# The low part of each weight block by a negating copy and an accumulating transfer, in a one-core diffusion step

## The chip, the cores and the metric

The kernel runs on one core of one Trainium2 chip. The metric is the device time in microseconds. Three runs of the kernel before took 1739.32, 1740.16 and 1740.61 us, so its time is the median, 1740.16 us.

## The reference

The reference is one inference step of a hybrid backbone with two layers (model width 1024, 512 latent and 128 context tokens, all in float32). Only its large products matter here; the mixers between the two projections (a gated delta rule in chunks, a spatial gating, a pooling) are left out.

```python
h = rmsnorm(x, norm1_g) * (1 + sc1) + sh1
cols = h @ w_in                      # 1024 x 2832, three groups of heads behind it
x = x + g1 * (concat(ya, yb, yc) @ w_out)      # 1024 x 1024
h = rmsnorm(x, norm2_g) * (1 + sc2) + sh2
gate, up = split(h @ w_gu)           # 1024 x 5632
x = x + g2 * ((silu(gate) * up) @ w_down)      # 2816 x 1024
```

The modulation (sh, sc, g) is a product of SiLU of a condition vector with w_mod (1024 x 6144 in each layer), once for the context and once for the latent tokens.

## The kernel before

All 640 tokens are kept transposed: features on the 128 partitions, tokens along the row. A product runs on 128 output features at a time. Its weight block is 1024 x 128 (768 x 128 in the last third of w_down), brought to one tile of 128 partitions with 8 (or 6) blocks side by side. The tokens go through in two halves of 320 columns.

TensorE multiplies float32 in a reduced form (float32r), so each operand is kept as two parts, hi and lo, whose sum is the value. A product is three passes: hi by hi, hi of the weights by lo of the tokens, lo of the weights by hi of the tokens (`mm3`, line 335). The lo part of a weight block, `wl`, is thus first needed by the third pass of the first block.

`wblock` (line 329) brings a block in and splits it. `wload` (line 297) issues the load of the raw weights into `w32` (called w in the profile) on SP's queue, all weight loads in the order of the program. `wsplit_` (line 311) then makes the parts: ScalarE casts the raw tile into `wh` (line 322); VectorE subtracts wh from the raw weights for the first 5 blocks (or 3), GpSimd for the last 3 (`GW`), into `wl` (lines 324 to 326; VectorE's operations all show as line 122). There are two buffers each of w32, wh and wl (`W32`, `WHL`). A buffer of wh or wl is written again when TensorE has done the last product that reads it, one of w32 when the subtractions have read it.

The modulation is worked off in small steps between the products (`pump_`, line 257): a load of 128 x 512 weights on SP's queue (line 268), a multiply-add on VectorE, a scaling on ScalarE in place, an addition on GpSimd (line 282) that also frees the buffer. There are three such buffers (`WM`). In the trace the additions all lie before 810 us, in the first layer.

The order on each engine's queue comes from the order of the program, moved by offsets (`at`, `PRI`; "split" is 70 earlier). Every engine takes its queue in order, and an instruction that waits holds up those behind it. The layers come one after the other: input projection with the mixers, output projection, feed-forward with 44 gate and up pairs in three pieces, each followed by its part of w_down.

Of the kernel before, what the change touches and what calls it, by code (L numbers as in the profile page):

```python
# [10 lines left out]
F32R = mybir.dt.float32r  # L11
# [6 lines left out]
P = 128  # L18
# [14 lines left out]
# steps of the modulation after each half of a product, by branch  # L33
PUMPS = {'log0': (0, 0), 'k00': (0, 0), 'q00': (1, 2), 'sgu0': (1, 1), 'z0': (0, 1), 'v10': (1, 1), 'q10': (0, 0), 'v00': (1, 0), 'k10': (0, 1), 'pool0': (1, 0)}
# engines of single steps: a ScalarE, v VectorE, p GpSimdE
ENG = {"gul11": "a", "kd10": "a", "conv_k01": "a", "conv_v10": "v", "gul00": "v", "mtc10": "v", "pumpmix0": "a", "kd11": "v", "gul01": "v", "mtc01": "a", "conv_q00": "v", "conv_v00": "v", "kd00": "a", "conv_q10": "a", "conv_k00": "v", "conv_q11": "a", "conv_v01": "a", "conv_v11": "a", "gul10": "a", "kn11": "a", "kn01": "a", "msb": "v", "pumpout0": "a", "dec01": "a", "conv_k11": "a", "dec00": "s", "pumpffn0": "a", "mtc11": "v", "mtc00": "a", "kd01": "a"}
GW, NB = 3, 2
# offsets in the order of issue: > 0 earlier
PRI = {"first": 1000, "rst": 80, "inverse10": 2000, "queries11": -230, "po": 240, "opost00": 180, "chain00": -220, "keys00": 530, "values00": -420, "br0": 200, "prep01": -170, "split": 70, "opost10": -30, "prep10": 430, "values11": 220, "chain11": 1000, "chain10": 10, "inverse01": 420, "keys10": 200, "evac": -10, "opost11": 50, "chain01": -300, "keys11": -100, "queries10": 130, "kept": -1000, "conv": -70, "br1": 10, "add": -100, "opost01": 100, "prep00": 50, "inverse11": -10, "values10": -30}
W32, WM, WHL = 2, 3, 2  # L40
# [5 lines left out]
def host_constants():  # L46
    f = np.float32
    p = np.arange(P)
    cols = {}
    cols["ones"] = np.ones((P, P), f)  # L50
    cols["U0"] = (p[:, None] <= p[None, :]).astype(f)
    cols["U1"] = (p[:, None] >= p[None, :]).astype(f)
    r, q = p[:, None] % 32, np.arange(32)[None, :]
    cols["MK"] = ((r >= 16) != (q >= 16)).astype(f)
    cols["I16"] = (p[:, None] % 16 == np.arange(16)[None, :]).astype(f)
    cols["m16"] = np.stack([p % 32 < 16, p % 32 >= 16], 1).astype(f)
    # from here on: not kept on chip as they are
    cols["ident"] = np.eye(P, dtype=f)
    cols["NID"] = np.eye(P, dtype=f) * f(NEG)
    cols["V0"] = (p[:, None] > p[None, :]).astype(f)  # L60
    cols["V1"] = (p[:, None] < p[None, :]).astype(f)
    quarter = D // 4
    omega = (f(1.0) / (f(10000.0) ** (np.arange(quarter, dtype=f) / f(quarter)))).astype(f)
    rr = np.arange(NL // GRID_W, dtype=f)[:, None] * omega
    cl = np.arange(GRID_W, dtype=f)[:, None] * omega
    row = np.concatenate([np.sin(rr), np.cos(rr)], -1).astype(f)
    col = np.concatenate([np.sin(cl), np.cos(cl)], -1).astype(f)
    for k in range(4):
        cols[f"row{k}"] = np.ascontiguousarray(row[:, k * P:(k + 1) * P].T)
        cols[f"col{k}"] = np.ascontiguousarray(col[:, k * P:(k + 1) * P].T)  # L70
    for nm, seg in (("l", GRID_W), ("c", P)):
        for g, win in enumerate(POOL_WINDOWS):
            b = np.zeros((P, P), f)
            for t in range(P):
                s0, pos = t // seg * seg, t % seg
                lo = min(max(pos - win // 2, 0), seg)
                hi = min(max(pos + win - win // 2, 0), seg)
                b[t, s0 + lo:s0 + hi] = f(1) / f(hi - lo)
                b[t, t] -= f(1)
            cols[f"B{nm}{g}"] = np.ascontiguousarray(b.T)  # L80
    off, o = {}, 0
    for k, v in cols.items():
        off[k] = (o, v.shape[1])
        o += v.shape[1]
    return np.ascontiguousarray(np.concatenate(list(cols.values()), axis=1)), off
# [6 lines left out]
def tile_hybrid_step(ctx: ExitStack, tc: tile.TileContext,  # L92
# [40 lines left out]
    def times(key, o, i, c, default):  # L133
        """o = i * c, c one number per row"""
        e = ENG.get(key, default)
        if e == "a":
            act(o, i, AF.Copy, scale=c)
        elif e == "v":
            ts(o, i, c, None, MUL)
        else:  # L140
            nc.gpsimd.tensor_scalar(o, i, c, None, op0=MUL)
# [10 lines left out]
    class at:  # L152
        """the instructions inside come that much earlier in the order of issue"""
# [11 lines left out]
    def behind(ins, prev):  # L165
        """queues one instruction of an engine behind another"""
        if prev is not None:
            tc.add_manual_dep(ins, prev.name, mybir.DependencyInfo(mybir.DependencyClass.NoSync,
                                                                   mybir.DependencyReason.DATA), reason="queue order")
# [7 lines left out]
    def in_turn(key, ins):  # L177
        """instructions of one kind in the order of the program"""
        behind(ins, recent.get(key))
        recent[key] = ins  # L180
# [38 lines left out]
    # steps: 512 columns x 128 rows of w_mod; a step's load is issued some steps ahead of its arithmetic  # L219
# [4 lines left out]
    def mod_sums(l, c0, ma):  # L224
# [11 lines left out]
        # sums over the 32 rows of each quarter, then over the quarters  # L236
# [50 lines left out]
    def pump_to(l, w):  # L287
        """until that sixth of the modulation is there"""
        n = 2 * KT * (SIXTHS.index((l, w)) + 1)
        while ps_["i"] < n:  # L290
            pump()
        if ps_["i"] == n and ps_["due"] is not None:
            mod_sums(*ps_["due"])
            ps_["due"] = None

# [1 line left out]
    def wload(parts, kn, n):  # L297
        """parts: [(dram [rows, n], k0, kn)] -> [P, kn, n]"""
# [7 lines left out]
    def wsplit(v):  # L306
        """hi, lo as blocks [P, n]"""
        with at("split"):
            return wsplit_(v)

    def wsplit_(v):
        kn, n = v.shape[1:]
        wh = wp.tile([P, 1024], F32R, tag="wH", name="wh", bufs=WHL)
        wl = wp.tile([P, 1024], F32R, tag="wL", name="wl", bufs=WHL)
# [8 lines left out]
        c = kn - GW  # L323
        tt(wl[:, 0:c], v[:, 0:c], wh[:, 0:c], SUB)
        if GW:
            nc.gpsimd.tensor_tensor(wl[:, c:], v[:, c:], wh[:, c:], op=SUB)  # L326
# [13 lines left out]
    def mmk(o, wb, k, xk, sl):  # L340
        """one k block of the products with the scaled residual; 16 columns: hi and lo in one operand"""
# [6 lines left out]
    def gemm_xs(wb, xs, evac, pumps=(1, 1), done=None):  # L348
        """products with the scaled residual; the first half carries two shift columns in front.
        done: the second half's, where it came first."""  # L350
# [28 lines left out]
    def rsqrt(y, a, t):  # L379
        """y = 1 / sqrt(a) for small tiles: bit shift, then three Newton steps; t: scratch like y."""  # L380
# [8 lines left out]
    class Norm:  # L389
        """scaled residual split in two, and the row statistics of the plain one."""  # L390
# [33 lines left out]
        def rstd(self, after=None):  # L424
            """per row: [row in chunk, chunk]"""
# [30 lines left out]
    wsp = tc.alloc_tile_pool(name="wsh", bufs=1, side="right")  # L456
    with tc.tile_pool(name="xin", bufs=1) as xp:
# [27 lines left out]
        def first_w(pool, j, c0, kp=KT):  # L485
            """512 columns of w_mod; the row blocks from kp on in the tiles of the later steps"""
# [7 lines left out]
        def first_mod(ws, c0, pool=None):  # L494
            """four row blocks side by side"""
            with at("first"):
                first_mod_(ws, c0, pool)
# [38 lines left out]
        # feature rows, positions added  # L536
# [35 lines left out]
        for k in range(KT):  # L572
# [5 lines left out]
            # sums of squares in two strands  # L578
# [18 lines left out]
    # ================= layers =================  # L597
    for l in range(DEPTH):
        xs = nrm.xs
        with ExitStack() as es:  # L600
            pa_, pb_ = (es.enter_context(tc.tile_pool(name=f"{t}{l}", bufs=1, reuse_waits="tile")) for t in ("ma", "mb"))
            # what the scans leave first lies where the residual comes back to
# [3 lines left out]
            if l == 0:  # L606
                # until the shift is there: halves of the first products that don't carry it
# [5 lines left out]
                def kept(w, t, c0):  # L613
                    """split into the tiles t, from column c0 of the first (hi) and the third (lo) on"""
# [79 lines left out]
            # beta = 1 / (1 + exp(-x)), kept negated  # L694
# [5 lines left out]
            # g = -exp(a_log) * softplus(alpha + dt_bias)  # L700
# [53 lines left out]
            def row_sums(b, so, i, t, dst=None):  # L754
                """sums of squares over each row of t; its natural layout in dst"""
# [10 lines left out]
            def keys(b):  # L766
# [6 lines left out]
                # kst: norm of k, its inverse square, and what the q norm leaves in the eps of the output norm  # L773
# [39 lines left out]
            # unit u = d * 10 + chunk * 2 + head  # L813
# [48 lines left out]
            def inverse(b):  # L862
                """MT holds -M^T (M strictly lower / upper); becomes (I + M)^-T in place."""
# [23 lines left out]
                for j in range(15):  # L887
# [7 lines left out]
                    else:  # L895
                        # few columns: float32 itself
# [4 lines left out]
                # forward units: Z = Y blocks; backward units: Z = X blocks  # L901
# [10 lines left out]
                # 16 -> 32: a forward and a backward unit share a tile, on different halves of its rows  # L912
# [27 lines left out]
                # diagonal 32-blocks of the result  # L940
# [5 lines left out]
                # 32 -> 64: forward and backward units share columns, on different partitions  # L946
# [32 lines left out]
                # 64 -> 128  # L979
# [21 lines left out]
            def chain(b):  # L1001
# [5 lines left out]
                for s in range(NCH):  # L1007
# [11 lines left out]
                    # scaled k, natural layout  # L1019
# [18 lines left out]
                    # (context units: vw = -v_new)  # L1038
# [73 lines left out]
            def to_nat(src, dst):  # L1112
                """two transposed tiles [128 ch, tokens] -> natural [128 tok, (chunk, 256)] in dst (two tiles of 3, 2 chunks)."""
# [9 lines left out]
            def mixt():  # L1123
                """tiles for the operands of the output projection, in place of what the scans have left."""
# [156 lines left out]
        mark(f"out{l}")  # L1281
        with tc.tile_pool(name=f"fx{l}", bufs=1, reuse_waits="tile") as xpool, tc.tile_pool(name=f"ft{l}", bufs=1, reuse_waits="tile") as ftp, tc.tile_pool(name=f"ff{l}", bufs=1, reuse_waits="tile") as fp:
# [25 lines left out]
            for pi_, fn in enumerate(pieces):  # L1308
# [23 lines left out]
                elif last:  # L1332
                    # back to natural layout, the final norm's statistics on the way
# [5 lines left out]
                    # both parts of the tokens use the same weights; they stay in tiles that the gate left  # L1339
# [97 lines left out]
```

## Time and profile before

| | before |
|---|---|
| median of the runs | 1740.16 us |
| profiled execution, first to last instruction (span) | 1737.7 us |
| TensorE busy | 1666.4 us (96%) |
| VectorE busy | 1155.2 us (66%) |
| ScalarE busy | 761.1 us (44%) |
| GpSimd busy | 585.3 us (34%) |
| mean granted TensorE clock | 0.987 |
| transfers of GpSimd's queue | 1152 packets, 2.51 MB |

The profile is of one execution. The runs were timed without it; the span lies 2.5 us under their median. PE is TensorE's matrix products, PEld its weight loads, DVE VectorE, ACT ScalarE, POOL GpSimd, SP the engine that only issues transfers; a q behind an engine means its queue. Products follow each other every 0.15 us while each is shown with some 0.31 us, since they overlap. An arrow in brackets names what ended an engine's idle time.

### The profile page before, as it was taken

How to read it: one execution, taken by the hardware profiler on the slowest of the kernel's cores; microseconds unless marked ns; L12 is line 12 of the kernel's file. 1: busy time of each engine (PE TensorE's matmuls, PEld its weight loads, DVE VectorE, ACT ScalarE, POOL GpSimd, SP SyncE). 2: the span in 40 equal slices, each digit the busy share in tenths (PEclk: the TensorE clock that was granted, in tenths of full speed). 3: DMA queues.
4: the chain of work that ended last, by engine and by line, in shares of the span. 5: the costliest groups of instructions: out<-in, count | busy, mean ns of one | idle time of the engine just before them, and what ended most of it. 6: DMA issues, size and time to landing. Idle time of an engine off the chain costs nothing.

```text
span 1737.7 us, 33153 instructions
## 1 busy us (share of the span) xinstructions
PE 1666.4 (96%) x12952; PEld 1603.2 (92%) x12952; DVE 1155.2 (66%) x2462; ACT 761.1 (44%) x1564; POOL 585.3 (34%) x578
## 2 busy tenths in 40 slices
PE   6999999998899999999999999999999999999997
PEld 4788989988899999999998899999999999999997
DVE  6698688799888688877467777675544434433454
ACT  4557765554444344434246656543322212321232
POOL 3342330367645454554164112013411221222110
PEclk8999999999999999999999999999999999999999
DMA  9431231444444544453241211113222222222221
GB/s 316 143 98 57 68 99 29 150 127 139 145 141 141 154 137 143 143 158 103 62 144 52 62 38 50 37 51 126 83 73 74 79 79 74 74 73 73 74 85 61
DMA packets 243379, 174.34 MB, mean 100 GB/s; under 512 B 10006, under 2 KB 212376, under 8 KB 243224
## 3 DMA queue, kind: packets, MB, share of 16 engines
q1 hardware_dynamic: 231888, 157.44, 29.8%
q10 hardware_dynamic: 10184, 12.29, 2.2%
q0 software_dynamic: 1152, 2.51, 0.4%
q8 instruction: 102, 1.67, 0.4%
q14 instruction: 53, 0.43, 0.1%
HBM read 163.29 MB, written 8.91 MB: 99 GB/s over the span
## 4 chain that ended last, share of the span: by engine, by line
PE 53%; DVE 3%; ACT 1%; issue 1%; POOL 0%; DMA 0%; DVEq 0%; POOLq 0%; ACTq 0%
PE acc L117 47%; PE dl L117 5%; DVE wl L122 0%; PE md L117 0%; DMA w<-in_w_down_dram 0%; PE dl L1379 0%; DVE cv L125 0%; POOL guh L830 0%; PE md L760 0%; DVE yt L125 0%; DVE st L125 0%; DVE Z L122 0%; ACT wh L322 0%; ACT MT L945 0%; DVE SI L122 0%
## 5 line engine op out<-in xcount | busy, mean ns | idle before, releaser
L117 PE MATMUL acc<-xhi,wh 128*128 128x322 f32 (+2 forms) x2112 | 667.4, 316 | 5.4 <-DVE ga L122 4.6
L117 PE MATMUL acc<-xlo,wh 128*128 128x322 f32 (+2 forms) x2112 | 666.0, 316 | 1.4 <-DVE xlo L125 1.2
L117 PE MATMUL acc<-xhi,wl 128*128 128x320 f32 (+1 forms) x2080 | 655.0, 315 | 5.1 <-DVE wl L122 5.1
L326 POOL TENSOR_TENSOR wl<-w,wh 128x384 fp32r<-128x384 f32 x188 | 258.7, 1376 | 792.5 <-ACT wh L322 777.9
L117 PEld LDWEIGHTS acc<-xhi,wh 128*128 128x128 f32 (+1 forms) x2112 | 399.4, 189 | 10.7 <-PE acc L117 7.2
L117 PEld LDWEIGHTS acc<-xlo,wh 128*128 128x128 f32 (+1 forms) x2112 | 400.2, 189 | 4.1 <-POOL spp L1148 1.5
L117 PEld LDWEIGHTS acc<-xhi,wl 128*128 128x128 f32 x2080 | 396.4, 191 | 6.6 <-DVE wl L122 5.9
L322 ACT CAST wh<-w 128x1024 fp32r<-128x1024 f32 (+1 forms) x188 | 194.5, 1035 | 343.4 <-PE acc L117 282.6
L282 POOL TENSOR_TENSOR ma<-ma,wm 128x512 f32<-128x512 f32 x140 | 207.2, 1480 | 133.5 <-ACT wm L150 113.8
L122 DVE TENSOR_TENSOR wl<-w,wh 128x640 fp32r<-128x640 f32 (+1 forms) x188 | 213.3, 1134 | 50.5 <-ACT wh L322 23.9
L117 PE MATMUL acc<-ah,wh 128*128 128x320 f32 (+2 forms) x632 | 195.6, 309 | 0.7 <-ACT ah L1322 0.7
L117 PE MATMUL acc<-al,wh 128*128 128x320 f32 (+2 forms) x632 | 195.1, 309 | 0.1
L117 PE MATMUL acc<-ah,wl 128*128 128x320 f32 (+2 forms) x632 | 195.1, 309 | 0.0
L150 ACT ACTIVATE wm<-wm,sc 128x512 f32<-128x512 f32 x140 | 101.1, 723 | 135.0 <-DVE ma L125 117.8
L125 DVE SCALAR_TENSOR_TENSOR x<-acc,mod,x 128x128 f32<-128x128 f32 (+3 forms) x192 | 77.9, 434 | 119.8 <-PE acc L117 119.5
L125 DVE SCALAR_TENSOR_TENSOR ma<-wm,sc,ma 128x512 f32<-128x512 f32 x140 | 134.9, 964 | 25.6 <-DMA wm<-in_w_mod_dram 24.7
L117 PEld LDWEIGHTS acc<-ah,wh 128*128 128x128 f32 x632 | 118.7, 188 | 1.2 <-ACT ah L1322 1.1
L117 PEld LDWEIGHTS acc<-al,wh 128*128 128x128 f32 x632 | 118.7, 188 | 0.3 <-DVE al L122 0.3
L117 PEld LDWEIGHTS acc<-ah,wl 128*128 128x128 f32 x632 | 118.7, 188 | 0.0
L1322 ACT CAST ah<-ga 128x320 fp32r<-128x320 f32 x88 | 40.5, 460 | 155.9 <-DVE ga L125 155.9
L150 ACT ACTIVATE ga<-ga,bt 128x320 f32<-128x320 f32 x132 | 57.4, 468 | 89.9 <-DVE ga L122 89.9
L122 DVE TENSOR_TENSOR ga<-acc,rst 128x320 f32<-128x320 f32 x88 | 42.4, 483 | 73.9 <-PE acc L117 73.4
(369 smaller groups left out, 2481.7 us busy)
## 6 DMA issues: line engine op xcount, KB each, us to landing
w<-in_w_gu_dram SPq DMA_DIRECT2D x88, 512.0 KB, 3.7
wm<-in_w_mod_dram SPq DMA_DIRECT2D x162, 256.0 KB, 2.9
w<-in_w_in_dram SPq DMA_DIRECT2D x44, 512.0 KB, 3.6
w<-in_w_down_dram SPq DMA_DIRECT2D x32, 512.0 KB, 4.2
w<-in_w_out_dram SPq DMA_DIRECT2D x32, 256.0 KB, 3.0
wf<-in_w_mod_dram SPq DMA_DIRECT2D x30, 256.0 KB, 6.5
w<-in_w_down_dram SPq DMA_DIRECT2D x16, 384.0 KB, 3.4
x<-xd ACTq DMA_DIRECT2D x16, 320.0 KB, 4.7
```

Of the source, the lines that this page charges most:

```text
L117: return nc.tensor.matmul(o, lhsT=l, rhs=r, start=st, stop=sp, **kw).ins
L122: recent["v"] = nc.vector.tensor_tensor(o, a, b, op=op).ins
L125: recent["v"] = nc.vector.scalar_tensor_tensor(o, a, s, b, op0=op0, op1=op1).ins
L150: recent["a"] = nc.scalar.activation(o, i, f, **kw).ins
L282: nc.gpsimd.tensor_tensor(ma[:, 1], ma[:, 1], wm, op=ADD)
L322: nc.scalar.copy(wh, v)
L326: nc.gpsimd.tensor_tensor(wl[:, c:], v[:, c:], wh[:, c:], op=SUB)
L1322: nc.scalar.copy(hi[:, sl], ga[:, sl])
```

## The change

In `wsplit_` the two subtractions go. ScalarE, behind the cast, copies the raw weights a second time with a scale of -1 into wl, which is float32r like wh and so holds minus hi. Then a transfer issued by GpSimd adds the raw tile to wl, from SBUF to SBUF. The number of buffers of wl has a name of its own (`WL`) and stays two. The other lines of the diff drop comments.

```diff
-GW, NB = 3, 2
+NB = 2
...
-W32, WM, WHL = 2, 3, 2
+W32, WM, WHL, WL = 2, 3, 2, 2
...
-        wl = wp.tile([P, 1024], F32R, tag="wL", name="wl", bufs=WHL)
+        wl = wp.tile([P, 1024], F32R, tag="wL", name="wl", bufs=WL)
...
         nc.scalar.copy(wh, v)
-        c = kn - GW
-        tt(wl[:, 0:c], v[:, 0:c], wh[:, 0:c], SUB)
-        if GW:
-            nc.gpsimd.tensor_tensor(wl[:, c:], v[:, c:], wh[:, c:], op=SUB)
+        act(wl, v, AF.Copy, scale=-1.0)
+        nc.gpsimd.dma_start(wl, v, accum_op=ADD)
         return tuple([t[:, k, :] for k in range(kn)] for t in (wh, wl))
```

## Rows read from the trace of the kernel before

**Rows 1.** The page, part 1: busy us, share of the span, instructions.

```profile
PE 1666.4 (96%) x12952; PEld 1603.2 (92%) x12952; DVE 1155.2 (66%) x2462; ACT 761.1 (44%) x1564; POOL 585.3 (34%) x578
```

**Rows 2.** The page, part 4: the chain that ended last, share by engine.

```profile
PE 53%; DVE 3%; ACT 1%; issue 1%; POOL 0%; DMA 0%; DVEq 0%; POOLq 0%; ACTq 0%
```

**Rows 3.** Windows: length, busy of PE, PEld, DVE, ACT, POOL (count), clock, DMA share, GB/s.

```profile
390.00:520.00 130.00, 117.98 (x774) 113.84 (x773) 115.38 (x175) 58.38 (x94) 79.42 (x61) 0.97 0.46 142
...
1210.00:1670.00 460.00, 459.26 (x3102) 458.02 (x3101) 199.32 (x392) 123.52 (x192) 106.61 (x81) 1.00 0.25 75
450.00:470.00 20.00, 16.50 (x107) 16.21 (x104) 18.84 (x27) 8.74 (x14) 11.92 (x9) 0.91 0.49 156
```

**Rows 4.** Windows of line 322 (the cast) alone: length, ACT busy (count), clock, DMA.

```profile
1210.00:1670.00 460.00, 68.06 (x65) 1.00 0.25 75
```

**Rows 5.** Order of time, quiet stretch, ACT and PE: start, length, engine, instruction.

```profile
1321.23 1.05 ACT L322 CAST wh<-w 128x1024 fp32r<-128x1024 f32 x1 [1.80 <-PE acc L117]
1328.36 1.05 ACT L322 CAST wh<-w 128x1024 fp32r<-128x1024 f32 x1 [2.29 <-PE acc L117]
1320.99 0.31 PE L117 MATMUL acc<-xhi,wl 128*128 128x320 f32 x1
1328.56 0.31 PE L117 MATMUL acc<-xhi,wl 128*128 128x322 f32 x1
```

**Rows 6.** Order of time, quiet stretch, POOL and DVE.

```profile
1322.36 1.07 POOL L326 TENSOR_TENSOR wl<-w,wh 128x384 fp32r<-128x384 f32 x1 [5.48 <-ACT wh L322]
1322.46 1.64 DVE L122 TENSOR_TENSOR wl<-w,wh 128x640 fp32r<-128x640 f32 x1
1329.44 0.82 DVE L122 TENSOR_TENSOR wl<-w,wh 128x640 fp32r<-128x640 f32 x1 [0.49 <-ACT wh L322]
```

**Rows 7.** Windows of line 282 (modulation additions) alone: length, POOL busy (count), clock, DMA.

```profile
390.00:420.00 30.00, 8.92 (x8) 0.94 0.44 137
...
810.00:840.00 30.00, 0.00 (x0) 1.00 0.30 88
```

**Rows 8.** Order of time, stretch with the modulation, ACT and PE.

```profile
471.27 1.03 ACT L322 CAST wh<-w 128x1024 fp32r<-128x1024 f32 x1
472.21 0.72 ACT L150 ACTIVATE wm<-wm,sc 128x512 f32<-128x512 f32 x1
...
480.42 1.03 ACT L322 CAST wh<-w 128x1024 fp32r<-128x1024 f32 x1
474.96 0.42 PE L117 MATMUL acc<-xhi,wl 128*128 128x322 f32 x1 [1.29 <-DVE wl L122]
483.09 0.31 PE L117 MATMUL acc<-xhi,wl 128*128 128x322 f32 x1
```

**Rows 9.** The page, part 5: groups; busy us, mean ns, idle before and its end.

```profile
L326 POOL TENSOR_TENSOR wl<-w,wh 128x384 fp32r<-128x384 f32 x188 | 258.7, 1376 | 792.5 <-ACT wh L322 777.9
L122 DVE TENSOR_TENSOR wl<-w,wh 128x640 fp32r<-128x640 f32 (+1 forms) x188 | 213.3, 1134 | 50.5 <-ACT wh L322 23.9
```

**Rows 10.** The output's tile, 1714 to 1715; then the queues, 1714 to 1722 (three issues).

```profile
L1396 POOL DMA_DIRECT2D out_dram<-y x1: 590/590/590, 1714.4 to 1714.4; - x1
DMA to landing us min/median/max: 3.0/3.0/3.0
q0 software_dynamic: 432, 1.57, 50.1%
```

**Rows 11.** The page, part 6: transfers, KB each, median us from issue to landing.

```profile
w<-in_w_in_dram SPq DMA_DIRECT2D x44, 512.0 KB, 3.6
wf<-in_w_mod_dram SPq DMA_DIRECT2D x30, 256.0 KB, 6.5
```

**Rows 12.** Waits of SP's queue, 390 to 630: us in total, times, longest.

```profile
SPq L268 <- POOL ma L282: 107.0, 59, 4.4
```

**Rows 13.** Order of time, input projection of the first layer, ACT and PE.

```profile
218.78 1.03 ACT L322 CAST wh<-w 128x1024 fp32r<-128x1024 f32 x1
222.78 0.40 PE L117 MATMUL acc<-xhi,wl 128*128 128x322 f32 x1
```

## The prediction, made before the changed kernel was run

> **What bounds the kernel now.** I read the page's busy table first, then the chain that ended last. TensorE is busy in 1666.4 of 1737.7 us, the other engines in 66%, 44% and 34% [rows 1]. TensorE holds 53% of the chain, VectorE 3%, ScalarE 1%, GpSimd nothing [rows 2]. So the 71 us in which TensorE is idle are all that any relief could give back, and work taken off VectorE and GpSimd is worth only what it takes out of those. The change can cost more than that: each weight block is split in two before TensorE can use it, and there are two buffers for each part. So I went to the order of time and measured the room between the cast of a block and the first product with its low part.
>
> The quiet stretch, 1210 to 1670 us, leaves TensorE no gap (459.3 of 460 busy [rows 3]) and holds 65 casts [rows 4]. A block's last product with wl starts at 1320.99, the cast into the freed buffer at 1321.23, and the first product with the new low part at 1328.56; the next cast follows 7.13 us after the first [rows 5]. Today both subtractions are over by 1324.1. The reader is to see there that VectorE's part takes 1.64 us where GpSimd's had started just ahead of it, and 0.82 in the next block [rows 6]: the two engines hold each other up.
>
> The stretch with the modulation, 390 to 810 us, is different: each window of 30 us has 7 to 10 of its GpSimd additions, and from 810 there are none [rows 7]. The casts stand on ScalarE among steps that wait for modulation weights: casts at 471.27 and 480.42, first products with their low parts at 474.96 and 483.09 [rows 8]. Before the first of these TensorE stood 1.29 us for the low part already. The room there is nearly used up.
>
> **The change part by part.** *Removed:* 188 subtractions on GpSimd (258.7 us) and 188 on VectorE (213.3 us) [rows 9]. The relief is valued below.
>
> *Added on ScalarE:* 188 negating copies of the cast's size. A cast takes 1.05 us [rows 5]; scaling is the same kind of pass, so I take 1.05, and a start 0.94 after the cast's, as the operation behind a cast has it (471.27, 472.21 [rows 8]). It stands ahead of the transfer, so all of it is in a block's latency. It also adds 197 us, 26% of ScalarE's 761.1; of the 1% of the chain that it holds (17 us) that is +5.
>
> *Added on GpSimd:* 188 issues. One takes 0.59 us [rows 10], less than the 1.38 that it replaces [rows 9]. It waits for the negating copy, and the modulation additions are queued behind it as they are behind the subtraction today; the copy ends about 1 us after the cast, so they are let go at about the same time. Free.
>
> *Added as a transfer:* 512 KB from SBUF to SBUF with an addition. No row shows one. From below: a plain 512 KB transfer of GpSimd's queue with nothing ahead of it lands 3.0 us after its issue; three of them keep the 16 engines 50.1% of 8 us busy, 1.34 us each [rows 10], so some 1.7 us do not depend on the size. An addition has to read both operands: 1.34 more, 4.3 in all. From above: the slowest large group of loads, 256 KB each at the crowded start, lands in 6.5 [rows 11]. I take 4.3, since the plain transfer of the same size is the nearest row; the ends are 3.0 and 6.5.
>
> *Moved:* the raw tile w becomes free when the transfer has landed, so SP's next weight load goes out later, and the modulation loads queued behind it on SP too; these already stand 107.0 us from 390 to 630 for the GpSimd additions that free their buffers [rows 12]. In the quiet stretch this is covered: a raw tile comes round every 14.25 us, and load 3.6 [rows 11], cast and copy 2.0 and transfer 4.3 make 10. In the modulation stretch I count it in the choice between the two prices below.
>
> **The sum at 4.3 us.** Quiet stretch: cast at 1321.23, copy over at 1323.22, issue 0.08 later (as GpSimd starts at 1322.36 where the cast ended at 1322.28 [rows 5, 6]), low part needed at 1328.56: room 5.25. The transfer fits with 0.95 to spare: 0 us. Each us beyond 5.25 would cost half a us per block, as two buffers share it.
>
> Modulation stretch: the issues come at 473.34 and 482.49, so the rooms are 1.6 and 0.6 [rows 8], short by 2.7 and 3.7. If the second cast is not late itself, the first delay covers part of the second and the pair costs 3.7; if SP makes it late, 6.4. I take 3.7 for each of 14 windows of 30 us [rows 7]: +52. A stall also takes clock: in the window from 450 to 470, with 3.5 us of idle, TensorE was granted 0.91, a level between 1.2 and 2.4 GHz on the mean [rows 3]. For half the windows 0.09 of the 16.5 us busy: 7 x 1.5 = +10.
>
> Input projections: a cast at 218.78 with the product at 222.78 [rows 13] leaves room 1.9, short by 2.4. Most blocks there have more, as products wait among the scans' small ones. I take one in six of the 44 loads [rows 11]: 7 x 2.4 = +17.
>
> Relief: 213.3 of VectorE's 1155.2 us go, 18% of the 3% of the chain that it holds (52 us): -10; with ScalarE's +5, -5.
>
> Together 52 + 10 + 17 - 5 = +74. The span of 1737.7 becomes 1812; the median of the runs is 2.5 above the span, so 1814 us.
>
> **The rivals.** *A: the transfer is slow, and the quiet stretch pays too.* It decides from 5.25 us on. Pieces of 512 B in place of whole rows of 4 KB, or weight loads beside it, would do it. At the upper end, 6.5: 65 x (6.5 - 5.25) / 2 = 41; modulation 14 x 8 = 112 (5.9 for the pair, 2 for the other blocks of the window, then short as well); projections 7 x 4.6 + 7 x 2 = 46; clock 20; relief -5: +214, 1954 us. For it: no row has an adding transfer. Against it: 0.95 us of margin by the plain one.
>
> *B: faster.* In the modulation stretch the casts are late because SP's modulation loads wait for GpSimd's additions [rows 12], which stand behind GpSimd's subtractions and run against VectorE. Without the subtractions the additions end sooner, the loads go out sooner and the casts come earlier. From 3.7 us earlier on nothing is short there, and TensorE gains half of the 12 us that it is idle from 390 to 520 [rows 3] (the other half is the norm) and 10 from the relief, less 4 left in the projections: -12, 1728 us. Against it: SP's weight load waits longer, and the modulation loads with it.
>
> *C: no change.* The same half-way: casts 2 us earlier, a transfer at 3.0, and the projections' rooms seldom used, within 3.5 us of 1740.
>
> *D: the issue is held up.* Rows 6 show VectorE and GpSimd blocking each other. If an issue waits for one VectorE operation of 0.8 us, the landing is at 5.1: the quiet stretch just fits; modulation 14 x 4.5 = 63, projections 7 x 3.2 = 22, clock 14, relief -5: +94, 1834 us. The Trainium skill ("SBUF — State Buffer", section "SBUF: two separate sides") has this as a rule: GpSimd writes the descriptors of its queue's transfers itself, and can't while VectorE runs an operation in a two-port mode. By it the time is D's, without it the forecast's; the trace agrees as far as one operation in each other's way goes (0.82 against 1.64), and its few issues from GpSimd ran with little beside them.
>
> **How the numbers follow.** My forecast has 0.50, A 0.28, D 0.06, C 0.05, B 0.11. Faster by over 0.2% (3.5 us, about what a measurement of this kernel can tell from no change) is B: 0.11; within it C: 0.05; slower the rest: 0.84. Below 1742 lie B and most of C, 0.13; above 1960 the slow end of A, 0.07: the range is 1742 to 1960. The forecast's own case spans 1781 (3.0 us: pairs 14 x 2.4, projections 7, clock 5) to 1885 (5.0 us and both of a pair paid: 14 x 7.8, projections 21, clock 20).
>
> **What would show it.** The landing of the new transfers: about 4.3 us, under 5.25 in the quiet stretch; in A over it. The quiet stretch: casts still 7.13 apart and TensorE without a gap; in A they stretch and TensorE waits for the transfer in each block. The waits: TensorE for the transfer into wl some tens of times, mostly from 390 to 810; none there means B. GpSimd's issue near 0.6 us; several us would mean many small pieces, and a length that goes with VectorE's work means D. By stretch: the modulation longer by about 60 us, the projections by about 17, the quiet one by nothing. I am wrong if the landing is over 5.25 us, or if the modulation stretch does not grow.

## The result, and the profile after

The changed kernel takes 1798.44 us, median of 4 runs (1793.94 to 1799.64), against 1740.38 for the kernel before, also 4 runs: a ratio of 1.0324, 95% interval 1.0309 to 1.034, slower by 58 us. The forecast was 1814. The profiled execution has a span of 1797.9 us.

The page of the changed kernel: busy times, the load of GpSimd's queue, the chain by engine, the groups that answer to [rows 2, 9], and the transfer's size and median landing.

```profile
PE 1682.5 (94%) x12952; PEld 1606.3 (89%) x12952; DVE 927.3 (52%) x2274; ACT 922.5 (51%) x1748; POOL 465.1 (26%) x578
...
q0 software_dynamic: 28224, 99.78, 29.3%
...
PE 57%; DMA 22%; DVE 7%; ACT 6%; issue 4%; POOL 3%; SPq 0%; ACTq 0%; POOLq 0%; DVEq 0%
...
L325 POOL DMA_DIRECT2D wl<-w x188 | 163.9, 872 | 995.4 <-ACT wl L150 851.6
...
L150 ACT ACTIVATE wl<-w 128x1024 fp32r<-128x1024 f32 (+1 forms) x188 | 195.9, 1042 | 20.7 <-DMA w<-in_w_in_dram 20.6
...
wl<-w POOLq DMA_DIRECT2D x178, 512.0 KB, 4.9
```

VectorE is 228 us less busy than in [rows 1], GpSimd 120 us less, ScalarE 161 us more, and the DMA share of the chain went from 0% [rows 2] to 22%, of which 14 are the new transfer's on the same page. The transfer is the new link. TensorE waits for it 50 times, at products that read a new low part:

```profile
PE acc L117 <- DMA wl<-w: 54.3, 50, 4.0
```

To see where, I cut both spans at the same events of the program: the first output projection of layer 0, the last modulation addition, the last product of layer 0's feed-forward network (FFN), the first output projection of layer 1. The third column is the kernel of experiment 1, which has the negation but no transfer. (us, each from its own profile.)

| stretch | before | after | without the transfer | after - before | the transfer alone |
|---|---|---|---|---|---|
| start and layer 0's projections | 333.1 | 347.8 | 335.7 | +14.7 | 12.1 |
| modulation | 470.8 | 488.7 | 443.1 | +17.9 | 45.6 |
| rest of layer 0's FFN | 100.7 | 107.8 | 102.4 | +7.1 | 5.4 |
| layer 1's projections | 279.9 | 281.3 | 275.1 | +1.4 | 6.2 |
| quiet stretch and end | 553.2 | 572.3 | 550.5 | +19.1 | 21.8 |
| sum | 1737.7 | 1797.9 | 1706.8 | +60.2 | 91.1 |

The quiet stretch, which had no gap in [rows 3], now has some. Windows of the kernel before, then of the changed one, over the modulation's stretch and the last one (columns as in [rows 3]):

```profile
333.10:803.90 470.80, 449.80 (x3030) 439.29 (x3029) 391.78 (x584) 204.47 (x313) 263.14 (x195) 0.99 0.47 144
1184.50:1737.70 553.20, 539.37 (x3627) 532.60 (x3625) 250.24 (x511) 157.36 (x310) 118.92 (x94) 0.99 0.26 79
```

```profile
347.80:836.50 488.70, 451.30 (x3025) 437.42 (x3024) 303.33 (x523) 257.63 (x372) 217.44 (x194) 0.99 0.79 203
1225.60:1797.90 572.30, 546.00 (x3627) 534.08 (x3625) 175.12 (x442) 219.59 (x379) 73.55 (x94) 0.99 0.59 140
```

TensorE's idle time goes from 21.0 to 37.4 us in the first and from 13.8 to 26.3 in the second. VectorE has far less to do in both.

One late block of the quiet stretch, in order of time: ScalarE and GpSimd, then TensorE.

```profile
1497.40 1.05 ACT L322 CAST wh<-w 128x1024 fp32r<-128x1024 f32 x1 [2.27 <-PE acc L117]
1498.35 1.06 ACT L150 ACTIVATE wl<-w 128x1024 fp32r<-128x1024 f32 x1
1499.70 0.86 POOL L325 DMA_DIRECT2D wl<-w  x1 [6.88 <-ACT wl L150]
...
1504.58 0.31 PE L117 MATMUL acc<-xlo,wh 128*128 128x322 f32 x1
1505.69 0.41 PE L117 MATMUL acc<-xhi,wl 128*128 128x322 f32 x1 [0.80 <-DMA wl<-w]
```

The cast starts where a buffer comes free. The issue stands 2.30 us behind it, where I had counted 2.07 (1.99 until the copy is over, 0.08 more): it comes 0.29 us after the negation ends. With the low part due 7.3 us after the cast, the room is about 5.0 us, where I had put 5.25. This transfer landed 5.95 us after its issue. The last 3.1 us of it, from the same trace (strip of DMA load in 40 slices, then GB/s, then queues with packets, MB and share of 16 engines):

```profile
DMA  0799209950014000400000300020000000000000
GB/s 0 211 317 423 53 0 317 370 106 0 0 0 53 0 0 0 53 0 0 0 0 0 53 0 0 0 53 0 0 0 0 0 0 0 0 0 0 0 0 0
...
q0 software_dynamic: 50, 0.14, 24.8%
q8 instruction: 1, 0.02, 1.8%
```

After 1503.6 us (slice 9) only single pieces move, 53 GB/s in a slice of 0.078 us, 4 KB each, one after the other; the last begins at 1505.0. One packet of instructions (1.8% of 16 x 3.1 us is 0.89 us) had run beside them, from 1503.0. The reading is that one engine had both, so that its share of the transfer comes in last and the whole transfer is late by it; the trace doesn't name a packet's engine, so this is inferred. I counted the 45 transfers issued from 1420 to 1740 us. Beside 19 of them such a packet ran between issue and landing, and 9 of these took over 5.0 us, up to 6.0. Of the 26 others 2 did, up to 5.3, both beside a weight load. That is a correlation read from the trace.

### The profile page after: what moved, and what is told of

Same layout as the page of the kernel before. It is cut to its first block, busy times and chain, and to the rows that moved or that the text cites. A ratio compares the mean times of both kernels' runs of the same rounds, so it can differ in the third digit from the quotient of the medians.

```text
span 1797.9 us, 33052 instructions
## 1 busy us (share of the span) xinstructions
PE 1682.5 (94%) x12952; PEld 1606.3 (89%) x12952; DVE 927.3 (52%) x2274; ACT 922.5 (51%) x1748; POOL 465.1 (26%) x578
## 3 DMA queue, kind: packets, MB, share of 16 engines
q0 software_dynamic: 28224, 99.78, 29.3%
## 4 chain that ended last, share of the span: by engine, by line
PE 57%; DMA 22%; DVE 7%; ACT 6%; issue 4%; POOL 3%; SPq 0%; ACTq 0%; POOLq 0%; DVEq 0%
PE acc L117 47%; DMA wl<-w 14%; PE dl L117 8%; DMA wm<-in_w_mod_dram 5%; DVE ma L125 2%; ACT wl L150 2%; POOL ma L282 2%; ACT wh L322 1%; DMA wf<-in_w_mod_dram 1%; DMA w<-in_w_in_dram 1%; ACT wm L150 1%; PE md L117 1%; PE md L759 0%; DMA w<-in_w_down_dram 0%; DVE cv L125 0%
## 5 line engine op out<-in xcount | busy, mean ns | idle before, releaser
L325 POOL DMA_DIRECT2D wl<-w x188 | 163.9, 872 | 995.4 <-ACT wl L150 851.6
L282 POOL TENSOR_TENSOR ma<-ma,wm 128x512 f32<-128x512 f32 x140 | 193.8, 1384 | 115.0 <-ACT wm L150 106.9
L150 ACT ACTIVATE wl<-w 128x1024 fp32r<-128x1024 f32 (+1 forms) x188 | 195.9, 1042 | 20.7 <-DMA w<-in_w_in_dram 20.6
L361 DVE COPY bt<-acc 128x2 f32<-128x2 f32 (+1 forms) x134 | 20.9, 156 | 177.3 <-PE acc L117 176.9
```

The source lines that it names most:

```text
L150: recent["a"] = nc.scalar.activation(o, i, f, **kw).ins
L282: nc.gpsimd.tensor_tensor(ma[:, 1], ma[:, 1], wm, op=ADD)
L325: nc.gpsimd.dma_start(wl, v, accum_op=ADD)
L361: nc.vector.tensor_copy(bt, o[:, 0:2])
```

## The experiments

Each was timed beside the kernel before on the same chip; a ratio is to that.

**1. The transfer left out.**

```
   act(wl, v, AF.Copy, scale=-1.0)
-  nc.gpsimd.dma_start(wl, v, accum_op=ADD)
```

> The accumulating transfer is left out, so wl holds minus hi alone; ScalarE's negating copy stays, and the subtractions stay away. Theory (what costs is the time from ScalarE's copy to the landing, 4.5 us and more, against a room of 5.25): all stalls for wl go, blocks in the quiet stretch follow each other at 7.13 us again, and the relief of VectorE and GpSimd shows alone: 1722 to 1740 us. Rival 1 (ScalarE's second pass and the changed order of its queue cost): the input projection of the first layer stays some 10 us longer, 1750 to 1775 us. Rival 2 (the relief is worth nothing, all of it is transfer): exactly 1740.

1708.23 us (1707.29 to 1708.87), ratio 0.9817 (0.9802 to 0.9831). So the transfer costs 90 us (1798.4 - 1708.2), and the relief that goes with the change, ScalarE's negation included, is worth 31 us, not the 5 that I had counted. 27.7 of it lie in the modulation's stretch:

```profile
335.70:778.80 443.10, 437.78 (x3018) 431.69 (x3017) 291.39 (x523) 254.85 (x370) 169.92 (x134) 1.00 0.50 151
```

TensorE's idle time is 5.3 us there against 21.0, and the same products take 12 us less, with the clock granted in full (1.00 for 0.99).

**2. The negation written ahead of the cast.**

```
-  nc.scalar.copy(wh, v)
   act(wl, v, AF.Copy, scale=-1.0)
   nc.gpsimd.dma_start(wl, v, accum_op=ADD)
+  nc.scalar.copy(wh, v)
```

> Same work, but ScalarE makes minus hi first and the cast behind it, so the transfer can go out some 0.95 us earlier and its room in the quiet stretch is 6.2 instead of 5.25 us. Theory (latency): landings stay 4.5 to 6, nearly all now fit, and the 24 us lost between the output projection of the second layer and the end go: 1765 to 1780 us. Rival (bandwidth or the transfers' traffic itself slows TensorE or the loads): no change, 1795 to 1800 us.

1797.81 us (1785.42 to 1803.63), ratio 1.0322 (1.0276 to 1.0369): as the changed kernel. It says nothing on the order, because the planner put the cast first all the same, as its order of time on ScalarE shows:

```profile
1505.38 1.05 ACT L324 CAST wh<-w 128x1024 fp32r<-128x1024 f32 x1 [1.73 <-PE acc L117]
1506.33 1.05 ACT L150 ACTIVATE wl<-w 128x1024 fp32r<-128x1024 f32 x1
```

**3. The same transfer as a plain copy**, without the addition.

```
-  nc.gpsimd.dma_start(wl, v, accum_op=ADD)
+  nc.gpsimd.dma_start(wl, v)
```

> The transfer copies the raw weights over wl without the addition (wl is then the raw weights): same issue, same bytes written, one operand read in place of two. Theory (the second operand's read is the addition's price): landing 3.1 to 3.4 us uncontended instead of 4.5, nothing short in the quiet stretch, 1735 to 1760 us. Rival (writing the descriptors, or the fixed part, sets the landing): landing stays above 4.2 us, 1785 to 1800 us.

1741.04 us (1737.2 to 1747.13, 10 runs), ratio 1.0013 (0.9999 to 1.0028). Of the 90 us, 57 belong to the addition and 33 to there being a transfer at all. Its page:

```profile
q0 software_dynamic: 28224, 99.78, 16.1%
...
L325 POOL DMA_DIRECT2D wl<-w x188 | 103.7, 552 | 1001.7 <-ACT wl L150 780.8
...
wl<-w POOLq DMA_DIRECT2D x178, 512.0 KB, 2.9
```

The same bytes in the same number of packets land in 2.9 us against 4.9, and the issue takes 552 ns against 872. The engines' time for one transfer, less the 0.5% of the queue that the kernel of experiment 1 still has, is (16.1% x 1738.5 - 8.5) / 188 = 1.44 us on all 16 engines; with the addition (29.3% x 1797.9 - 8.5) / 188 = 2.76. The Trainium skill ("Collectives: The Full Stack", section "The bandwidth ceiling: the fold count and why AG ≠ RS ≠ AR") says of the adding step of a collective that it is slower because the addition needs two source reads, not because the adding costs cycles. Here the engines' time is 1.91 times the copy's, which agrees with twice the reading; no run separates the reading from the adding.

By stretch, the modulation's and then the quiet one with the end:

```profile
340.50:802.20 461.70, 446.29 (x3033) 437.47 (x3032) 302.13 (x524) 257.67 (x373) 204.15 (x194) 0.99 0.67 215
1184.80:1738.50 553.70, 539.18 (x3627) 532.63 (x3625) 175.22 (x442) 219.58 (x379) 50.95 (x94) 0.99 0.44 144
```

Against the kernel without a transfer, the copy costs 18.6 us in the first (443.1) and only 3.2 in the second (550.5), where the adding transfer costs 21.8. A landing of 2.9 us lies well inside the room of 5.0.

**4. Only GpSimd's three blocks by negation and transfer**; VectorE subtracts its five as before.

```
-  act(wl, v, AF.Copy, scale=-1.0)
-  nc.gpsimd.dma_start(wl, v, accum_op=ADD)
+  c = kn - 3
+  act(wl[:, c:], v[:, c:], AF.Copy, scale=-1.0)
+  nc.gpsimd.dma_start(wl[:, c:], v[:, c:], accum_op=ADD)
+  tt(wl[:, 0:c], v[:, 0:c], wh[:, 0:c], SUB)
```

> Only GpSimd's three of the eight row blocks go the new way (negating copy and accumulating transfer of 192 KB); VectorE subtracts the other five as before. Theory (latency, proportional part): landing 1.8 + 3/8 x 2.7 = 2.8 to 3.0 us, copy 0.45, so ready 0.7 + 2.9 after the cast: fits everywhere but in the tightest pairs: 1735 to 1755 us. Rival (fixed cost of any transfer from GpSimd's queue rules): landing over 4 us, 1775 us or more.

1730.85 us (1728.13 to 1734.71), ratio 0.9949 (0.9928 to 0.9969): faster than both kernels. The transfer is of 192 KB and lands sooner; TensorE waits for it 5 times, 7.3 us in all, where it was 50 times and 54.3:

```profile
wl<-w POOLq DMA_DIRECT2D x188, 192.0 KB, 3.0
```

**5. The cast queued behind the negation on ScalarE**, which experiment 2 had not reached.

```
-  nc.scalar.copy(wh, v)
   act(wl, v, AF.Copy, scale=-1.0)
+  neg = recent["a"]
   nc.gpsimd.dma_start(wl, v, accum_op=ADD)
+  behind(nc.scalar.copy(wh, v).ins, neg)
```

> The changed kernel, with the cast to the high part queued behind the negation on ScalarE, so that the transfer is issued about one cast (0.94 us) earlier in a window; nothing else is changed. Theory (the landing is late only because 4.5 us of transfer barely fit in a room of 4.9 to 5.0 us): the room grows to about 5.9 us, more than nearly all landings in the quiet stretch, and the 24 us that the quiet stretch lost go, with part of the 18 us of the modulation stretch: 1755 to 1785 us. Rival (the lost time is DMA traffic, which the order on ScalarE doesn't change): 1795 to 1800 us. A second rival (the cast, now later, becomes what the first products wait for): 1800 us or more.

1812.78 us (1808.2 to 1816.12), ratio 1.0412 (1.0393 to 1.043). As a forecast of the time the theory missed. The time is in the second rival's range, but not by its mechanism: TensorE waits for the cast only twice, 1.8 us in all. By stretch the theory held where it was made for, and something else came up elsewhere. Quiet stretch and end, then the modulation's stretch:

```profile
1250.90:1808.70 557.80, 539.98 (x3627) 532.67 (x3625) 175.16 (x442) 219.78 (x379) 74.35 (x94) 0.99 0.61 143
...
347.40:860.10 512.70, 463.87 (x3022) 450.77 (x3021) 288.21 (x523) 256.31 (x370) 217.11 (x194) 0.96 0.75 192
```

The quiet part takes 557.8 us against 572.3 with the cast first and 553.2 before: 14.5 of the 19.1 us come back with 0.9 us more of room, at the same size of transfer and nearly the same landings (median 4.5 against 4.6). That is more than one profile differs from the next: the same stretch took 577.4 us in experiment 2 and 576.0 in 12, both with the cast first there.

The stretch has layer 1's output projection in front and the end of the kernel behind it. The output projection took 62.5 us before, 71.5 with the change and 65.3 here. The feed-forward products behind it, before, with the change, and here:

```profile
1247.00:1676.20 429.20, 428.46 (x2890) 427.22 (x2890) 182.75 (x366) 112.31 (x177) 87.00 (x60) 1.00 0.25 74
...
1297.10:1737.40 440.30, 432.21 (x2892) 427.25 (x2891) 119.38 (x307) 166.10 (x235) 51.64 (x60) 1.00 0.63 145
...
1316.20:1745.30 429.10, 428.73 (x2891) 427.32 (x2890) 119.45 (x306) 166.05 (x234) 51.73 (x60) 1.00 0.64 148
```

There the whole loss of 11.1 us is gone. The same kind of block, issued early:

```profile
1496.30 1.06 ACT L150 ACTIVATE wl<-w 128x1024 fp32r<-128x1024 f32 x1 [2.39 <-PE acc L117]
1497.26 1.04 ACT L325 CAST wh<-w 128x1024 fp32r<-128x1024 f32 x1
1497.65 0.86 POOL L324 DMA_DIRECT2D wl<-w  x1 [6.26 <-ACT wl L150]
...
1503.52 0.31 PE L117 MATMUL acc<-xhi,wl 128*128 128x322 f32 x1
```

5.87 us from issue to need. The modulation's stretch is 24 us longer than with the cast first (512.7 against 488.7). What holds it, ScalarE and then VectorE in order of time:

```profile
657.46 0.55 ACT L150 ACTIVATE ga<-ga,bt 128x320 f32<-128x320 f32 x1
659.89 0.72 ACT L150 ACTIVATE wm<-wm,sc 128x512 f32<-128x512 f32 x1 [1.88 <-DVE ma L125]
660.52 1.05 ACT L150 ACTIVATE wl<-w 128x1024 fp32r<-128x1024 f32 x1
...
657.66 1.87 DVE L125 SCALAR_TENSOR_TENSOR ma<-wm,sc,ma 128x512 f32<-128x512 f32 x1 [0.45 <-DMA wm<-in_w_mod_dram]
```

The negation's buffer was free from 655.7, when the last product with the old low part started, but it starts at 660.5: ahead of it on ScalarE stands a scaling of the modulation, which waits for VectorE's addition, which had waited for a modulation load. TensorE then stood 3.25 us. Such stalls repeat every 33 us, and the clock fell to 0.96 over the stretch.

**6. GpSimd relieved, VectorE not**: no transfer, VectorE subtracts five blocks, the other three get minus hi only.

```
-  act(wl, v, AF.Copy, scale=-1.0)
-  nc.gpsimd.dma_start(wl, v, accum_op=ADD)
+  c = kn - 3
+  act(wl[:, c:], v[:, c:], AF.Copy, scale=-1.0)
+  tt(wl[:, 0:c], v[:, 0:c], wh[:, 0:c], SUB)
```

> No transfer; VectorE subtracts five of eight blocks as before, and the last three get minus hi from ScalarE and no raw weights (the low part of those blocks is left incomplete). Theory (the 31 us by which the kernel without any low-part work on VectorE and GpSimd beat the kernel before come from GpSimd's subtractions being gone, which take 4.0 us of a window's chain and hold GpSimd's modulation additions up): 1708 to 1715 us. Rival (they come from VectorE's load going down): 1730 to 1740 us. Both halves matter: 1715 to 1730 us.

1715.33 us (1712.96 to 1716.85), ratio 0.9853 (0.9839 to 0.9866): 25 us of experiment 1's 31.

**7. VectorE relieved, GpSimd not**, the mirror of it.

```
-  act(wl, v, AF.Copy, scale=-1.0)
-  nc.gpsimd.dma_start(wl, v, accum_op=ADD)
+  c = kn - 3
+  act(wl[:, 0:c], v[:, 0:c], AF.Copy, scale=-1.0)
+  nc.gpsimd.tensor_tensor(wl[:, c:], v[:, c:], wh[:, c:], op=SUB)
```

> The mirror of it: no transfer; GpSimd subtracts the last three blocks as before, and the first five get minus hi from ScalarE and no raw weights (the low part of those blocks is left incomplete). Theory (GpSimd's subtraction is what costs): 1733 to 1742 us, as before. Rival (VectorE's load is what costs): 1708 to 1715 us. Both halves matter: 1715 to 1730 us.

1729.36 us (1722.97 to 1731.3), ratio 0.9923 (0.9903 to 0.9944): 11 us. So both halves matter, and over the whole GpSimd's is worth more. By stretch it is otherwise. In the modulation's stretch the two are worth about the same: 470.8 us before, 453.5 in experiment 6, 450.1 here and 443.1 with both gone. Together the 17 and 21 us are more than the 28 of both, which fits that either removes the pairing of [rows 6]. What sets the experiments apart lies in the projections: layer 1's take 273.9 us in experiment 6 and 285.6 here, against 279.9 before. The group of each, VectorE's in experiment 6 and GpSimd's in experiment 7:

```profile
L122 DVE TENSOR_TENSOR wl<-w,wh 128x640 fp32r<-128x640 f32 (+1 forms) x188 | 166.7, 886 | 37.5 <-ACT wh L322 36.7
```

```profile
L325 POOL TENSOR_TENSOR wl<-w,wh 128x384 fp32r<-128x384 f32 x188 | 203.8, 1084 | 843.6 <-ACT wh L322 817.5
```

Beside each other they took 1134 and 1376 ns [rows 9].

**8. Experiment 4 with the cast behind the negation.**

```
-  nc.scalar.copy(wh, v)
   act(wl[:, c:], v[:, c:], AF.Copy, scale=-1.0)
+  neg = recent["a"]
   nc.gpsimd.dma_start(wl[:, c:], v[:, c:], accum_op=ADD)
+  behind(nc.scalar.copy(wh, v).ins, neg)
   tt(wl[:, 0:c], v[:, 0:c], wh[:, 0:c], SUB)
```

> The version in which only GpSimd's three blocks go by negation and accumulating transfer (1730.9 us), with the cast queued behind the negation on ScalarE. Theory (landing against room decides): its 2.95 us of transfer fitted in the room already, so the order gains little: 1727 to 1732 us. Rival (VectorE's subtraction, now one negation later, sets the first products): 1733 to 1742 us.

1734.02 us (1732.08 to 1736.67), ratio 0.9963 (0.995 to 0.9975). It lies in the rival's range, but the interval overlaps that of experiment 4, so that the rival isn't shown. What is seen is that the order on ScalarE gains nothing where the landing fits already.

**9. Experiment 5 with the negation, transfer and cast earlier in the order of issue.**

```
-  "split": 70
+  "split": 250
```

> The kernel with the cast forced behind the negation, and the pair (negation, transfer, cast) issued earlier in the order of work (offset 250 in place of 70), so that on ScalarE it stands ahead of the modulation's scaling. Theory (the 19 us that the forced order lost in the modulation stretch 562 to 837 us are negations queued behind a scaling that waits for VectorE, as at 655.7 to 660.5 us, and the quiet stretch's recovery stays): 1770 to 1795 us. Rival (that stretch is lost to the transfers' late landings whatever the order, and the clock falls with them): 1805 to 1815 us.

1816.66 us (1814.5 to 1821.51), ratio 1.044 (1.0425 to 1.0455). The time lies just above the rival's range, and the theory fell in this form: the offset did not lift the negation over the scaling. At 697.73 the same scaling, with the same wait of 1.9 us for VectorE, still stands ahead of a negation whose buffer had been free since 694.8. So the order at that place was not changed, and whether a better one would mend it stays open. The quiet part and end took 559.6 us, again near the 553.2 of before.

**10. All eight blocks on VectorE**, no transfer and no negation, in the kernel before.

```
-  GW, NB = 3, 2
+  GW, NB = 0, 2
```

> The kernel before with all eight blocks subtracted by VectorE, none by GpSimd; no transfer, no negation. It asks whether the gain of the version with three blocks by transfer (1730.9 us) is only that GpSimd no longer subtracts. Theory (GpSimd's subtraction was the slow piece; VectorE takes 3/5 more, about 1.0 us a window, mostly beside other work): 1715 to 1732 us. Rival (VectorE, 65% busy before, becomes the bound in the modulation stretch): 1740 to 1760 us.

1727.91 us (1724.8 to 1732.75, 6 runs), ratio 0.9929 (0.9914 to 0.9944), as the theory had it: the fastest version that computes everything, though not told apart from experiment 4. Eight blocks cost VectorE hardly more than five did beside GpSimd (213.3 us [rows 9]):

```profile
L122 DVE TENSOR_TENSOR wl<-w,wh 128x1024 fp32r<-128x1024 f32 (+1 forms) x188 | 246.5, 1311 | 44.8 <-ACT wh L322 43.8
```

So a gain like experiment 4's needs no transfer: what the two have in common is that GpSimd no longer subtracts.

**11. Half the weight loads in layer 1's FFN**, the other halves zeros.

```
+  if ps_["at"] == "ffn1" and kn == 8:
+      parts = [(parts[0][0][0:4 * P], 0, 4)]
+      nc.vector.memset(v[:, 4:8, :], 0.0)
```

> The changed kernel with half of each full weight block of layer 1's feed-forward (8 row blocks) left unloaded: those halves are zeros written by VectorE, so half of these weight loads' traffic is gone; the transfer keeps its 512 KB. Theory (late landings in this stretch come from 16 KB instruction packets on one engine, and from a room of 5.0 us with little to spare): the stretch keeps most of its loss of 10 to 14 us between 1296.8 and 1740.3 us; 1790 to 1800 us. Rival (they come from collision with the weight loads): landings of 4.5 us throughout, 1780 to 1788 us.

1797.61 us (1795.06 to 1804.5), ratio 1.0334 (1.0314 to 1.0354): no change, and the quiet part and end take the same 572.3 us (1796.4 less 1224.1). TensorE waits 12.8 us for the transfer there, against 13.5 in the changed kernel. So half of the weight loads' traffic is not what the loss hangs on. The landings of that stretch still reach 6.2:

```profile
DMA to landing us min/median/max: 3.9/4.5/6.2
```

**12. The same in layer 0's FFN**, beside the modulation (`ffn0` for `ffn1`).

> The changed kernel with half of each full weight block of layer 0's feed-forward (the layer beside the modulation) left unloaded, zeros written by VectorE in its place; the transfer keeps its 512 KB, layer 1 is as in the changed kernel. It is the same edit that changed nothing in layer 1, put where the loads of the modulation's weights share the engines. Theory (in this stretch the loss of 18 us is traffic: transfer, weight load and modulation load collide, the modulation's additions wait 58 us for their loads where they waited 16, and the negation stands behind them on ScalarE): 5 to 15 us of it come back, 1783 to 1793 us. Rival (it is the room of 5.0 us alone, as in layer 1): no change, 1795 to 1801 us.

1806.29 us (1805.22 to 1811.88), ratio 1.0375 (1.0357 to 1.0392). Neither expectation: it is slower than the changed kernel. In its stretch the traffic did what it should: VectorE's waits for modulation loads, from 562 to 837 us in the changed kernel,

```profile
DVE ma L125 <- DMA wm<-in_w_mod_dram: 58.3, 31, 3.2
```

went to 22.3 here (16.2 in the kernel before), and the transfers' median from 5.4 to 4.9 us. But the zeros had to wait for the raw tile that the transfer reads, and held VectorE up:

```profile
DVE w L303 <- DMA wl<-w: 35.9, 21, 3.3
DVE ma L125 <- DMA wm<-in_w_mod_dram: 22.3, 26, 3.2
```

The two make 58.2, so the wait may only have moved from the loads to the zeros. Nor is that wait a measure of the traffic: without any transfer (experiment 1) it is 38.7 us from 523.2 to 778.8. So it isn't shown that traffic makes the modulation's loads late. The modulation's stretch took 483.8 us against 488.7, with landings shorter by half a us. How much of the 45.6 us is traffic stays open.

The 8 us by which the whole is slower came later, in layer 1's projections (294.9 against 281.3 us). The expectation takes their code for the changed kernel's, but it isn't: the name in `ps_["at"]` stays `ffn0` until layer 1's output projection, so their blocks were half unloaded and filled with zeros too. From 939.5 to 1234.1 us:

```profile
L303 DVE MEMSET w<- 128x512 f32 x20 | 9.7, 485 | 35.5 <-DMA wl<-w 14.0 <-ACT on L1074 7.2 <-ACT MT L1001 5.3
```

VectorE stands idle 35.5 us before these 20 fills, which the changed kernel doesn't have. That is the likely cause of the 13.6 us; no run took the fills away. The whole time of this experiment therefore decides nothing between its theory and its rival.

## Why the prediction was right, and where not

**Landing time.** Counted as a copy with a second read, 4.3 us; the undisturbed landings are 4.5, the median over all is 4.9. The construction held (plain 2.9, one more read of 1.3 of the engines' time). It is a figure for a transfer with nothing beside it. In the modulation's stretch the median was 5.3, over the 5.25 that I had named for a sign of being wrong; over the whole run 12 of 188 landings took longer than rival A's 6.5, up to 7.6.

**Issue.** 0.59 us was a copy's; with the addition it is 0.87, and it comes 0.29 us after the negation instead of 0.08. "Free" held, as it is still less than the subtraction it replaced. Nothing of rival D: the issues are 856 to 901 ns long in the modulation's stretch, without VectorE's operations showing in them.

**Quiet stretch.** 0 us was wrong: 22 for the transfer alone. The step that failed is "The transfer fits with 0.95 to spare: 0 us". It compared the landing of an undisturbed transfer with the room; the issue ate 0.25 us and the landing 0.2, so that some 0.5 us were left, and the landings spread by more than that. Experiments 3 and 5 show it from both sides: with a landing of 2.9 us 18.6 of the 21.8 us went, and with 0.9 us more of room 14.5, among them all of the loss in the feed-forward products. So the quiet stretch did pay, as in rival A, though by half of A's 41 us. That instruction packets make the spread rests on the trace, and on experiment 11, where half the load traffic changed nothing; no run took the packets away. A third buffer for wl, for which the change has the name `WL`, would widen the room; no run tried it.

**Modulation stretch.** Predicted +52, and 10 of clock; the transfer alone cost 45.6 there, clock included: 32.1 more of idle time and 13.5 because the same products took longer (451.3 against 437.8). The place and the wait are right. The pattern is not: instead of 3.7 us once in each of 14 windows there are 24 waits of 1.3 us on the mean, 31.5 in all. The relief of that stretch, 27.7 us, hid most of it, so that the stretch grew by only 17.9. It did grow, as I had named for a sign, but by a third of the term.

**Relief.** This was the term mis-sized: -5 against -31. I had taken the share of VectorE's time on the chain over the whole run, 3%, and cut it down in proportion. What the subtractions cost was local: with them TensorE was 21 us idle and below the full clock in one stretch, and without them 5 us and at the full clock. The bound of 71 us had left out that relief gives clock back too: 12 of the 27.7 us are products that took less long.

This is where rival B had put a gain, at -12, but the path that B gave isn't what the traces show. B had SP's modulation loads wait less for GpSimd's additions. In the modulation's stretch they waited as long without the subtractions, while ScalarE's waits for VectorE's multiply-adds, which stand among the casts on its queue, were nearly halved. Before, then in experiment 1:

```profile
SPq L268 <- POOL ma L282: 192.6, 106, 5.1
ACT wm L150 <- DVE ma L125: 102.2, 62, 5.3
...
SPq L268 <- POOL ma L282: 197.1, 109, 4.0
ACT wm L150 <- DVE ma L125: 56.8, 34, 4.2
```

So the relief seems to come through VectorE and ScalarE, with the two engines out of each other's way. That is read from the traces; what experiments 1, 6 and 7 show is its worth, with ScalarE's negation, whose price by itself was not measured.

**Projections.** +17 predicted for both layers, +16.1 measured, 18.3 for the transfer alone. TensorE waited only 4.1 us for the transfer before the first output projection (from 37 to 348 us, 3 times), so the sum came out better than its reason: seven waits of 2.4 us are not what is there.

**Clock.** +10 predicted. From the mean granted clock, 0.987 before and 0.982 after, it is about 1797.9 x 0.018 - 1737.7 x 0.013 = 10 us (an estimate, as it takes the loss of clock for loss of time). It is not where I had put it: the modulation's stretch has 0.99 before and after, as the relief gave back there what the transfer took.

The sum: 79 for the transfer and -5 for the relief gave 74. The runs give 90 and -31, 58 together. Both terms were too small, by 11 and 26, in opposite directions. That the total came within 16 us is thus in part luck, and so is the nearness of the transfer's own term: 22 us of the quiet stretch and 5 of the first feed-forward were missing, and the modulation was 16 too high. Of the chances, 0.11 and most of 0.05 make some 0.15 below 1742 us, not 0.13.

## What to carry to other kernels

Measure an engine's relief in the stretch where its result is last, not by its share of the whole chain; leaving the work out altogether (experiments 1, 6 and 7) prices it in three runs. Before moving elementwise work to a transfer, compare room and landing with the spread of the landings, not their floor: half a us of margin on 5 did not hold, and a transfer of three eighths of the size cost little. Before reading a difference off an experiment, look where its edit reaches: a name that stayed set put experiment 12's zeros into a second place. And try first whether one engine can do the whole of a job that two share: here it did eight blocks in 16% more time than five beside the other engine.

## What the runs showed of the hardware

An accumulating transfer within SBUF costs the DMA engines 1.91 times the plain copy (2.76 against 1.44 us for 512 KB on 16 engines) and lands 1.6 us later undisturbed (4.5 against 2.9); GpSimd's issue of it takes 0.87 us against 0.55, whether for 512 KB or for 192 KB.

A transfer over 16 engines is as late as its last pieces: beside one packet of instructions of 0.9 us, the last 4 KB pieces of one transfer moved one after the other for about 1.4 us, and it landed after 5.95 us in place of 4.5.

VectorE's and GpSimd's subtractions, both with two inputs in SBUF, took 1134 and 1376 ns on the mean beside each other, 886 and 1084 apart. The Trainium skill ("SBUF — State Buffer", section "SBUF: two separate sides") says that such a pair takes a shared port in turn and whichever comes second waits out the other's whole instruction; in the quiet stretch before, the blocks with 1.64 us for VectorE's 0.82 [rows 6] show the same.
